# Bias tables asked for two heads ahead, and columns' rows with the last bias row, in a four-layer attention and recurrence trunk

## The chip, the cores and the metric

The kernel runs on one core of a Trainium2 chip. The metric is the device time of one execution in microseconds; of several executions the median counts. The engines are named as the profile names them: PE is TensorE (PEld its weight load), DVE is VectorE, ACT is ScalarE, POOL is GpSimd and SP is SyncE, here only a queue of DMAs.

## The reference

512 tokens of width 1024 go through two layers, each a token mixer and a gated feed-forward block (FFN) with a short convolution, all in float32, each between two RMS norms. The first layer's mixer is dilated attention with 8 heads in three groups, the second one's a gated linear recurrence (RG-LRU). What touches the change is the attention's bias and the convolutions' weights:

```python
m, valid, kidx = band_geometry(band)
bucket = t5_bucket(np.clip(m, 0, band) * dilation)
bias = jnp.transpose(bias_table.astype(jnp.float32)[bucket], (2, 0, 1))
...
logits = jnp.einsum('bxhnqd,bxhnkd->bxhnqk', qs, kk) * scale
logits = logits + bias[None, None, :, None]
mx = jnp.max(logits, axis=-1, keepdims=True)
p = jnp.exp(logits - mx)
s = jnp.sum(p, axis=-1, keepdims=True)
o = jnp.einsum('bxhnqk,bxhnkd->bxhnqd', p, vv) / s
```

A bias depends only on the distance of query and key, so that a head's bias is one row of numbers, shifted by one from query to query. The convolutions are depthwise: each channel has three (FFN) or four (recurrence) weights and a bias.

## The kernel before

Every float32 matrix is held as two float32r parts, a high one and the rest, and a product is three matmuls. The weights come from HBM in pieces of about 1 MB: `load` (L299) issues them on SP, ACT makes the high part (L240 in `pump`) and DVE the low one (L249 in `low_parts`). Eight such units may be live. For some products sums of two weight blocks are needed; `add_up` (L282) loads one block on SP (L292) and lets POOL add the other by an accumulating DMA into the same tile (L294).

The code is written in the order in which each engine works; no scheduler reorders it, and each engine keeps that order, so that an instruction that waits holds up all behind it on its engine. The order is interleaved by hand: after each block of matmuls, some 5.5 us of PE, `tick` (L351) lets every registered side generator take its next step and splits one or two weight units. A side's `yield n` means that it goes on n ticks later.

The attention (`attention`, L856) works through four pairs of heads twice. In the first round it projects queries, keys and values for group 0 and registers `local` (L1038) for two heads, which go on during the next pair's projections: in one tick the scores (PE, L1047), scores plus bias with their maximum (DVE, L1034) and exponentials (ACT, L1060); three ticks later the transposes (PE, L1069) and their copies; one tick later the product with the values (L1082). In the second round `strided` (L1089) does the same for groups 1 and 2 of a head together, and mixes the three groups.

The side `biases` (L864) runs in the first pairs. It makes for each of the three groups a row of bias values per head (matmul L875, copy L876, written to HBM at L877) and writes it 128 times into `skew` in HBM (L878), so that a DMA that reads it with a row step of one less than the row's length gets a head's bias table as a tile. `toeplitz` (L889) is that DMA, issued on POOL (L891) where a head's scores are emitted, into the tile `toe`, of which there are two buffers. After the third group `biases` loads three small constants and goes on into `feature_columns` (L705): it loads the convolutions' weights as rows (`column_rows`, L685, DMAs at L691 on SP), two ticks later turns them into columns by a PE transpose (`columns`, L695, transpose L698, copy L700), and for the recurrence computes constants from one of them by a chain of small DVE operations (L717 to L730). Then it does so for each of the two FFNs.

Most intermediate tiles are 128x512 float32 tiles of the pool `gp`, of which there are 30 buffers (`GEN_BUFS`). A tile's buffer is free after its last use, and a new tile takes a free one, the oldest as a rule. `dynamic_dma_scratch_size` (L1494) is the space in each SBUF partition in which POOL writes the descriptors of its DMAs, here 2048 bytes.

## Time and profile before

| | |
|---|---|
| median of 3 runs | 1486.01 us (1485.98 to 1488.6) |
| the profiled execution | 1485.73 us |
| its span, first to last instruction | 1484.0 us |
| PE busy | 1459.4 us (98%) |
| DVE busy | 931.1 us (63%) |
| ACT busy | 655.8 us (44%) |
| POOL busy | 78.0 us (5%) |
| mean granted TensorE clock | 0.994 |

All later times are microseconds from the span's start. The attention layer takes the first 540 us or so, the first FFN runs to about 930, the recurrence to about 1080, and the second FFN to the end. A row of the chain of waits has start, length and what ran; a row of the timeline has start, length, engine, line, operation, tiles (out<-in) and, in brackets, how long the engine sat idle before it and what ended that. A row of the windows has the stretch, then the busy time of PE, PEld, DVE, ACT and POOL with their counts, then granted clock, DMA share and GB/s. A releaser is inferred; where the engine named was done long before, it was another, often a DMA.

### The profile page before, as it was taken

The numbers are of one execution on the slowest core, as the hardware profiler recorded it, in microseconds if no ns is written. First come the engines' busy times: TensorE is split into PE (matmuls) and PEld (weight loads), VectorE is DVE, ScalarE is ACT, GpSimd is POOL, SyncE is SP. The second block draws the span as 40 slices with busy tenths as digits, with TensorE's granted clock in tenths as the row PEclk, the third lists the DMA queues.
The fourth block names the chain that finished last, engine by engine and source line by source line (L and its number), as shares of the span: only waits on it lengthen the run. The fifth ranks groups of instructions, "written<-read, shape, count | busy, mean of one in ns | idle before, by whom it ended". The sixth has DMA issues, their size and how long they took to land.

```text
span 1484.0 us, 19296 instructions
## 1 busy us (share of the span) xinstructions
PE 1459.4 (98%) x7625; PEld 1249.1 (84%) x7625; DVE 931.1 (63%) x1627; ACT 655.8 (44%) x1098; POOL 78.0 (5%) x91
## 2 busy tenths in 40 slices
PE   8999989999999999999999999999999999999998
PEld 6787868888888898999988888988798999888886
DVE  6365345255535588887877336877778888775333
ACT  5343234243434454454545224479554445544221
POOL 0101110111000000111000000000000011000000
PEclk9999989999999999999999999999999999999999
DMA  6664555736534343677645212331343667545101
GB/s 202 213 188 114 127 138 173 182 81 187 194 103 164 114 153 108 142 180 185 171 165 199 90 57 85 103 125 44 119 137 109 161 161 175 161 163 199 65 0 57
DMA packets 152651, 203.86 MB, mean 137 GB/s; under 512 B 5896, under 2 KB 129296, under 8 KB 152561
## 3 DMA queue, kind: packets, MB, share of 16 engines
q1 hardware_dynamic: 128064, 170.64, 34.2%
q0 software_dynamic: 24496, 31.99, 11.7%
q8 instruction: 60, 0.98, 0.3%
q14 instruction: 31, 0.25, 0.0%
HBM read 189.98 MB, written 17.34 MB: 140 GB/s over the span
## 4 chain that ended last, share of the span: by engine, by line
PE 85%; DVE 6%; ACT 4%; DMA 3%; issue 1%; SPq 0%; POOL 0%; DVEq 0%; ACTq 0%; POOLq 0%
PE ps L416 41%; PE acc L416 22%; PE vq L416 11%; PE vq L948 4%; PE v L922 2%; DVE wlo L249 2%; DVE xb L1286 1%; DMA raw<-in_attn_w_qkv_dram 1%; PE tr L465 1%; PE S L1111 1%; PE O L1082 1%; PE O L1179 1%; ACT whi L240 1%; PE S L1047 1%; DVE th L1338 1%
## 5 line engine op out<-in xcount | busy, mean ns | idle before, releaser
L416 PE MATMUL ps<-hT,whi 128*128 128x512 f32 (+1 forms) x2240 | 647.6, 374 | 0.8 <-ACT qk L902 0.7
L416 PEld LDWEIGHTS ps<-hT,whi 128*128 128x128 f32 x2240 | 405.7, 189 | 72.8 <-ACT qk L902 2.2
L416 PE MATMUL ps<-hT,wlo 128*128 128x512 f32 (+1 forms) x1120 | 416.7, 372 | 0.0
L249 DVE TENSOR_TENSOR wlo<-raw,whi 128x1024 fp32r<-128x1024 f32 x244 | 295.2, 1219 | 141.2 <-ACT whi L240 140.7
L240 ACT ACTIVATE whi<-raw 128x1024 fp32r<-128x1024 f32 x244 | 252.7, 1053 | 193.5 <-PE acc L416 124.4
L416 PEld LDWEIGHTS ps<-hT,wlo 128*128 128x128 f32 x1120 | 211.5, 189 | 37.2
L416 PE MATMUL acc<-whi,ahi 128*128 128x512 f32 x512 | 200.6, 392 | 1.1 <-ACT ahi L171 1.1
L416 PE MATMUL acc<-whi,alo 128*128 128x512 f32 x512 | 199.5, 390 | 0.0
L416 PE MATMUL acc<-wlo,ahi 128*128 128x512 f32 x512 | 199.2, 389 | 0.0
L750 DVE SCALAR_TENSOR_TENSOR u<-ps,cols,u 128x511 f32<-128x511 f32 (+1 forms) x128 | 95.7, 748 | 38.5 <-ACT u L746 36.2
L416 PEld LDWEIGHTS acc<-whi,ahi 128*128 128x128 f32 x512 | 96.1, 188 | 21.0 <-ACT ahi L171 1.5
L416 PEld LDWEIGHTS acc<-whi,alo 128*128 128x128 f32 x512 | 96.1, 188 | 20.6 <-DVE alo L172 0.4
L416 PEld LDWEIGHTS acc<-wlo,ahi 128*128 128x128 f32 x512 | 96.2, 188 | 19.5
L416 PE MATMUL vq<-T,whi 128*128 128x256 f32 x512 | 93.4, 283 | 0.0
L416 PEld LDWEIGHTS vq<-T,whi 128*128 128x128 f32 x512 | 81.4, 192 | 1.9
L240 ACT ACTIVATE whi<-sum 128x1024 fp32r<-128x1024 f32 x40 | 41.8, 1052 | 86.1 <-DMA sum<-in_attn_w_qkv_dram 60.6
L249 DVE TENSOR_TENSOR wlo<-sum,whi 128x1024 fp32r<-128x1024 f32 x40 | 48.5, 1220 | 44.8 <-ACT whi L240 44.8
L416 PE MATMUL vq<-T,wlo 128*128 128x256 f32 x256 | 72.4, 283 | 0.0
L760 ACT ACTIVATE u<-u 128x512 f32<-128x512 f32 x48 | 30.4, 632 | 92.2 <-DVE u L750 92.2
L416 PE MATMUL vq<-hT,whi 128*128 128x256 f32 x384 | 69.7, 283 | 0.0
L1034 DVE CUSTOM_DVE_ANT_0 L<-S,toe 128x128 f32<-128x128 f32 (+1 forms) x96 | 25.1, 320 | 63.4 <-DMA toe<-skew 31.3
L746 ACT ACTIVATE u<-ps,cols 128x512 f32<-128x512 f32 x64 | 49.0, 766 | 31.7 <-PE ps L416 31.7
(211 smaller groups left out, 1698.5 us busy)
## 6 DMA issues: line engine op xcount, KB each, us to landing
raw<-in_ffn_w_up_dram SPq DMA_DIRECT2D x40, 1024.0 KB
raw<-in_attn_w_qkv_dram SPq DMA_DIRECT2D x26, 1024.0 KB
raw<-in_ffn_w_down_dram SPq DMA_DIRECT2D x12, 1024.0 KB
raw<-in_ffn_w_down_dram SPq DMA_DIRECT2D x24, 512.0 KB
raw<-in_attn_w_qkv_dram SPq DMA_DIRECT2D x16, 512.0 KB
sum<-in_attn_w_qkv_dram POOLq DMA_DIRECT2D x16, 512.0 KB, 6.3
sum<-in_ffn_w_up_dram SPq DMA_DIRECT2D x16, 512.0 KB
sum<-in_ffn_w_up_dram POOLq DMA_DIRECT2D x16, 512.0 KB, 6.3
```

The source lines that it names most:

```text
L240: nc.scalar.activation(hi, raw, AF.Copy)
L249: nc.vector.tensor_tensor(lo, raw, hi.bitcast(F32), op=ALU.subtract)
L416: mm(dst, l[a], r[b], start=start and n == 0, stop=stop and n == 2)
L465: nc.tensor.transpose(ps[:, k * P : (k + 1) * P], xs[i][:, k * P : (k + 1) * P], ident)
L746: nc.scalar.activation(u, ps, AF.Identity, scale=cc[:, j : j + 1], bias=cc[:, 48 + j : 49 + j])
L750: nc.vector.scalar_tensor_tensor(u[:, d:], ps[:, : S - d], wc, u[:, d:], op0=ALU.mult, op1=ALU.add)
L760: nc.scalar.activation(u, u, AF.Gelu_apprx_tanh)
L922: mm(banks[t], hT[a][:, k, t * P : (t + 1) * P], W[b][:, k % 2, :], start=(k, a, b) == (0, 0, 0), stop=(k, a, b) == (KD - 1, 1, 0),)
L948: mm(banks[u], act(a)[:, 2 * j + k, u * P : (u + 1) * P], W[b][:, k, :], start=(j, k, n) == (0, 0, 0), stop=(j, k, n) == (1, 1, 2),)
L1034: nc.vector.tensor_tensor_reduce(dst, ps, bias, scale=1.0, scalar=3 * NEG, op0=ALU.add, op1=ALU.max, accum_out=mx)
L1047: mm(Sp[a // 2][:, o + lo : o + 256], q[hh][:, a * P : (a + 1) * P], k[hh][:, k0 : (a + 1) * P], start=True, stop=True)
L1082: mm(po[:, a * P : (a + 1) * P], pts[a, j], vtile(v, a - 1 + j, h % 4), start=j == js[0], stop=j == 1)
```

## The change

- `toeplitz` no longer loads one table into a tile that it is given. A list `tables` holds all 24 tables in the order of their use; each call asks for as many as there are buffers for (`TOE_BUFS`, now 3 instead of 2) and returns the oldest one asked. So the first call asks for three tables, and each later one for one table, two calls ahead of its use.
- The rows of the columns, all five tiles of them with their sixteen DMAs, are asked for in the step in which the third group's bias row is made (`g == 2`), four ticks earlier than the first ones before. `feature_columns` gets the loaded rows, and its ticks of waiting between loading and transposing are gone, so that the five transposes follow in three successive ticks.
- The general pool has 29 buffers instead of 30.
- The space for POOL's descriptors is 4096 bytes of each partition instead of 2048.

```diff
-GEN_BUFS = 30
-TOE_BUFS = 2
+GEN_BUFS = 29
+TOE_BUFS = 3
...
-    def feature_columns():
+    def feature_rows():
         v = lambda r: r.rearrange("(j p) -> j p", p=P)
         v2 = lambda r: r.rearrange("n (j p) -> (n j) p", p=P)
-        rows = column_rows(
+        yield column_rows(
             [(v(lru_conv_w[0, k]), 8) for k in range(4)]
             + [(v(lru_conv_b[0]), 8), (v2(lru_ga_b[0]), 8), (v2(lru_gx_b[0]), 8), (v(lru_lambda[0]), 8)]
         )
-        yield 2
-        cl = columns(*rows)
+        for layer in range(2):
+            cw, cb = ffn_conv_w[layer], ffn_conv_b[layer]
+            yield column_rows([(v(cw[0]), 48), (v(cw[1]), 48)])
+            yield column_rows([(v(cw[2]), 48), (v(cb), 48)])
+
+    def feature_columns(rows):
+        cl = columns(*rows.pop(0))
...
         for layer in range(2):
-            cw, cb = ffn_conv_w[layer], ffn_conv_b[layer]
-            rows = column_rows([(v(cw[0]), 48), (v(cw[1]), 48)]), column_rows([(v(cw[2]), 48), (v(cb), 48)])
-            yield 2
-            ffn_cols[layer] = [columns(*r) for r in rows]
+            ffn_cols[layer] = [columns(*rows.pop(0)) for _ in range(2)]
             yield 1
...
+                if g == 2:
+                    rows = list(feature_rows())
                 yield 3
...
-            yield from feature_columns()
-
-        def toeplitz(dst, g, h, n):
-            o = skew[g].offset + h * P * TOE + 127
-            nc.gpsimd.dma_start(dst, bass.AP(tensor=skew[g].tensor, offset=o, ap=[[TOE - 1, P], [1, n]]))
+            yield from feature_columns(rows)
+
+        tables = [(0, h, 256) for h in range(HEADS)]
+        tables += [(g, h, P) for h in range(6) for g in (1, 2)] + [(g, h, P) for g in (1, 2) for h in (6, 7)]
+        asked = []
+
+        def toeplitz(*which):
+
+            while tables and len(asked) < TOE_BUFS:
+                g, h, n = tables.pop(0)
+                T = gp.tile([P, 256], F32, tag="toe", name=nm("toe"), bufs=TOE_BUFS)
+                o = skew[g].offset + h * P * TOE + 127
+                src = bass.AP(tensor=skew[g].tensor, offset=o, ap=[[TOE - 1, P], [1, n]])
+                nc.gpsimd.dma_start(T[:, :n], src)
+                asked.append(((g, h), T))
+            key, T = asked.pop(0)
+            assert key == which
+            return T
...
         def local(h, hh, q, k, v):
-            T = gp.tile([P, 256], F32, tag="toe", name=nm("toe"), bufs=TOE_BUFS)
-            toeplitz(T, 0, h, 256)
+            T = toeplitz(0, h)
...
-                T = gp.tile([P, 256], F32, tag="toe", name=nm("toe"), bufs=TOE_BUFS)
-                toeplitz(T[:, :P], gi + 1, h, P)
+                T = toeplitz(gi + 1, h)
...
-    nc = _bacc.Bacc("TRN2", target_bir_lowering=False, num_devices=1, dynamic_dma_scratch_size=2048)
+    nc = _bacc.Bacc("TRN2", target_bir_lowering=False, num_devices=1, dynamic_dma_scratch_size=4096)
```

## The prediction

> **What bounds the kernel now.** I read the page first, then the list of PE's waits, then the chain of waits around each of them, and last the queues of the engines that the change touches.

> ```profile
> span 1484.0 us, 19296 instructions
> PE 1459.4 (98%) x7625; PEld 1249.1 (84%) x7625; DVE 931.1 (63%) x1627; ACT 655.8 (44%) x1098; POOL 78.0 (5%) x91
> PE PT L1069 <- ACT L L1060: 6.6, 1, 6.6
> PE cols L698 <- DMA st<-in_ffn_conv_w_dram: 2.2, 1, 2.2
> PE c L1165 <- DVE qk L904: 0.8, 1, 0.8
> ```

> The run is bound by TensorE: it idles 1484.0 - 1459.4 = 24.6 us, the most that an edit leaving its matmuls alone can win by idle time. Three of its few waits (time in all, count, longest) hang on what the diff touches: transposes of a local head's weights (L1069), transposes of the columns' rows (L698), and the small product at L1165 in the first strided head.

> Place one, by the chain of waits (start, length, what), with the last matmul ahead of it:

> ```profile
> 129.79 0.39 PE L922 MATMUL v<-whi,hT 128*128 128x512 f32 x1
> 125.18 5.10 DMA raw<-in_attn_w_qkv_dram
> 130.67 1.66 DMA st<-in_ffn_conv_w_dram
> 132.34 0.34 PE cols L698
> 132.68 1.69 PE PT L1069 x7
> 134.36 6.08 PE ps L416 x24
> 142.00 0.77 PE PT L1069 x7
> 142.76 5.47 PE ps L416 x24
> 132.00:134.00 2.00, 1.66 (x8) 1.57 (x9) 1.93 (x4) 0.93 (x2) 0.00 (x0) 0.53 0.14 37
> ```

> PE ends its value product at 129.79 + 0.39 = 130.18 and stands until the rows land (the chain hangs on the last of the small loads, which SP issued behind a 1 MB weight load). Afterwards the granted clock, the third number from the end in the window row, is 0.53: the same seven transposes and 24 matmuls take 1.69 and 6.08 us, and at full clock, eight us later, 0.77 and 5.47.

> Place two:

> ```profile
> 177.35 1.68 PE L1047 MATMUL S<-qk,qk 128*128 128x128 f32 x8
> 189.56 5.28 issue
> 194.85 0.76 POOL sum L294
> 195.60 5.74 DMA toe<-skew
> 201.48 0.29 DVE L1034 CUSTOM_DVE_ANT_0 L<-S,toe 128x128 f32<-128x128 f32 x1 [20.36 <-DMA toe<-skew]
> 203.05 1.97 ACT L L1060 x8
> 196.58 0.39 PE L416 MATMUL ps<-hT,wlo 128*128 128x512 f32 x1
> 203.60 2.16 PE L1069 MATMUL PT<-ident,L 128*128 128x128 f32 x7 [6.63 <-ACT L L1060]
> 206.50 7.69 PE ps L416 x24
> 204.00:206.00 2.00, 1.75 (x7) 0.86 (x6) 1.70 (x12) 2.00 (x7) 0.19 (x1) 0.50 0.22 66
> ```

> Head 4's scores S are there at 177.35 + 1.68 = 179.03. VectorE cannot add the bias: its table stands in GpSimd's queue behind two accumulating loads, the second of which starts only after 5.28 us without a visible releaser. The table lands after 201, VectorE has idled 20.36 us and blocked everything behind it, the exponentials follow, and PE stands from 196.97 to 203.60. Its clock is then 0.50.

> **The change part by part.** *Tables two heads ahead (three buffers).* Nothing is added: 24 table loads before and after. What moves is when they are asked for.

> ```profile
> 113.17 1.62 POOL L891 DMA_DIRECT2D toe<-skew  x2
> 141.32 1.33 POOL L294 DMA_DIRECT2D sum<-in_attn_w_qkv_dram  x1 [26.52 <-ACT qk L902]
> DMA to landing us min/median/max: 2.1/4.4/8.5
> 119.34 0.29 DVE L1034 CUSTOM_DVE_ANT_0 L<-S,toe 128x128 f32<-128x128 f32 x1 [10.97 <-PE S L1047]
> ```

> The call of head 2 will ask for head 4 and that of head 3 for head 5, where today the two tables of heads 2 and 3 are asked, at 113.17. With the longest landing, 8.5 us, head 4's table is there at about 122, 57 us before S. Head 4 at place two then runs: VectorE is done with the step before at 201.48 - 20.36 = 181.12, scores and maxima take 203.05 - 201.48 = 1.57, exponentials 1.97, done at about 184.7. PE wants them at 196.97, so 12 us are spare and the stall is gone. Without it, place two costs 0.77 + 5.47 = 6.24 us instead of (206.50 + 7.69) - 196.97 = 17.22: **11.0 us won**.

> Each new ask waits for the maxima of the call before it, whose buffer it takes. Queued behind it on GpSimd are the accumulating loads; the nearest one behind an early ask starts at 141.32, 28 us after 113.17, and at place two the two loads stand ahead of the asks. VectorE finishes a head's maxima 1.57 us after it starts them, so these waits cost nothing; if that cover went, an accumulating load would be late by what the wait lasts, and ACT, which splits in order, with it.

> Head 2 gains as well: VectorE's 10.97 us ahead of 119.34 end 6.2 us after its table was asked, which is the table's landing and not the later S that the row names. I count that at nothing, since PE works through it.

> The first strided head is the third place:

> ```profile
> 309.13 1.68 POOL L891 DMA_DIRECT2D toe<-skew  x2
> 316.26 0.29 DVE L1034 CUSTOM_DVE_ANT_0 L<-S,toe 128x128 f32<-128x128 f32 x1 [11.18 <-PE vq L948]
> ```

> Again the scores start a landing (7.1 us) after the ask, and VectorE's backlog runs from there into the 0.8 us wait at L1165. Tables asked during heads 6 and 7 take these 7 us out: **0.8 us won**.

> *Columns' rows with the last bias row.* Sixteen small loads move on SP, from behind the weight load of 125.18 (and two later places) to the step in which the third bias row is made.

> ```profile
> 83.73 0.37 SPq L322 DMA_DIRECT2D raw<-in_attn_w_qkv_dram  x1
> 92.84 0.37 SPq L322 DMA_DIRECT2D raw<-in_attn_w_qkv_dram  x1
> 130.67 1.24 SPq L691 DMA_DIRECT2D st<-in_ffn_conv_w_dram  x3
> 163.62 2.06 SPq L691 DMA_DIRECT2D st<-in_ffn_conv_w_dram  x3
> 104.13 2.00 ACT L240 ACTIVATE whi<-raw 128x1024 fp32r<-128x1024 f32 x2
> 134.96 0.22 DVE L700 COPY cols<-cols 128x64 f32<-128x64 f32 x1
> 138.75 0.17 DVE L730 TENSOR_SCALAR pad<-c 128x8 f32<-128x8 f32 x1
> ```

> In SP's order they fall between the weight loads of 83.73 and 92.84, where SP has 92.84 - 84.10 = 8.7 us free. An issue takes 1.24/3 = 0.41 to 2.06/3 = 0.69 us, sixteen 6.6 to 11.0, so the load of 92.84 and the loads behind it slip by 0 to 2.3 us. With a landing like the 5.10 us above it is there at 97.9 and ACT splits it from 104.13: 6.2 us cover the slip; what went beyond them would come out of ACT's and then PE's time. The rows are then read at the step of head 3's scores, about 117, twenty us after their issue. Place one costs 0.77 + 5.47, and 0.17 for the rows' own transpose at full clock, 6.41 us instead of (134.36 + 6.08) - 130.18 = 10.26: **3.9 us won**. VectorE's chain of small operations on these columns, 138.92 - 134.96 = 4.0 us, moves ahead of head 3's scores; VectorE is then earlier by the idle time ahead of 119.34, and head 3's transposes come only at 142.00, so it costs nothing.

> [...]

> *Descriptor space 4 KB.* If the 5.28 us are a wait for space, the second accumulating load starts right after the first and lands up to 5 us earlier. PE shows no wait for these sums, so I price it at 0; the bounds are 0 and, against, whatever two such loads at once take from a weight load, whose nearest row is again the 6.2 us of cover.

> *29 general buffers.* No instruction changes; an allocation takes a buffer freed one step later. I take 0; its upper bound is the second rival.

> **Sum.** 11.0 + 3.9 + 0.8 = 15.7 (unrounded 15.6). I keep back 0.6, somewhat less than one wait like that of L1165, because PE will reach everything behind 130 earlier than today: 15.0. The profiled execution took 1485.73 us, 1.73 outside its span; the median of the runs shown, 1486.01, is 0.28 above it. Forecast 1486.0 - 15.0 = **1471.0 us**.

> **The rivals.** *ACT's wait for the sums takes the table's place.* Behind head 5's exponentials ACT splits the summed tile and only then copies head 4's transposed weights.

> ```profile
> DMA to landing us min/median/max: 5.8/6.3/10.3
> ```

> If the larger space does nothing, the second load still starts at 194.85 and lands after 6.3 us at 201.1; a split like that of 104.13 (1.0 us) and the copy (about 0.5) follow at 202.6, and PE wants the copy 6.24 us after 196.97, at 203.2. That fits; with the longest landing, 10.3, PE would stand 3.4 us and lose as much as place one (1.7) by the clock: 1476. For it speaks that ACT idles on such sums elsewhere; against, that it needs two misfortunes. A slip of the rows that leaves place one as it is gives 1475. I give both together 0.16.

> [...] That the small loads behind an accumulating load are issued at once, and only a second accumulating one waits, speaks for space all the same.

> *Slower: the general buffers run out in the FFN.* Counted in the code from first to last use, general tiles reach 29 at once near the end of each FFN's up-projections, one below today's 30 and all of the new pool.

> ```profile
> L750 DVE SCALAR_TENSOR_TENSOR u<-ps,cols,u 128x511 f32<-128x511 f32 (+1 forms) x128 | 95.7, 748 | 38.5 <-ACT u L746 36.2
> 740.00:760.00 20.00, 20.00 (x123) 17.93 (x122) 15.64 (x22) 10.08 (x12) 0.00 (x0) 1.00 0.39 130
> ```

> If each of the last two pairs' evacuations (12 in a layer, 24 in all) waited one VectorE step of 0.75 us and PE with it, 18 us would be lost: 1471 + 18 = 1489. It decides where evacuation is as slow as PE; the window shows VectorE at 15.64 and ACT at 10.08 of 20 us beside a full PE, with eight PSUM banks between them. Chance 0.03.

> *Nothing changes:* another wait ends just as late at both places, some weight load behind ACT's order, and the time stays at 1486. Against it: at place two all of ACT and VectorE waits for this one table. Chance 0.05.

> **How the numbers follow.** The forecast, 1469 to 1473.5, has 0.76; the partial cases to 1477 have 0.16. The range 1469 to 1477 leaves out the last two rivals and some tails. A measurement here tells about 0.2%, 3 us, from no change; every case but the last two lies beyond it: faster 0.92, within 0.05, slower 0.03.

> **What would show it.** Right: the waits of L1069 and L698 gone from PE's list, the granted clock 1.00 from 130 to 140 and from 190 to 210, VectorE no longer waiting for toe, the row loads issued around 85 to 95, the pairs of accumulating loads 1 to 2 us apart. Wrong: a wait of PE behind ACT's split of a sum near 195, a weight load late near 100, or idle PE with half clock in the FFN around 780.

## The result, and the profile after

The changed kernel takes **1471.06 us** (median of 4 runs, 1470.15 to 1472.11) beside 1485.99 us for the kernel before on the same chip: a ratio of 0.9898, 95% interval 0.9881 to 0.9915. Its profiled execution took 1470.15 us. From its page (PE is busy for 1455.4 us, 99%) and its list of PE's waits (us in all, times, longest):

```profile
span 1468.4 us, 19295 instructions
...
PE tr L465 <- DVE xs L501: 2.0, 2, 1.8
...
PE acc L416 <- ACT ahi L171: 1.3, 1, 1.3
PE v L939 <- ACT hT L469: 1.1, 1, 1.1
PE c L1180 <- DVE s L1182: 0.2, 1, 0.2
```

All three places are gone from the list, and no wait has taken their part. (A line 15 to 17 above one of before is the same line.) Where the time was won shows at four products that both kernels do. Three rows of each kernel are from the chain of waits, in which a product starts some 0.16 us later than in the timeline (214.19 there, 214.03 here). Head 4's scores are compared in the timeline, where they start at 177.35 before. Before:

```profile
214.19 1.56 PE O L1082 x14
...
303.11 1.78 PE S L1111 x16
...
353.90 1.78 PE O L1179 x16
```

After:

```profile
131.25 0.77 PE PT L1085 x7
132.02 5.48 PE ps L416 x24
...
199.79 1.56 PE O L1098 x14
...
288.71 1.78 PE S L1126 x16
...
338.08 1.78 PE O L1194 x16
```

```profile
173.95 1.68 PE L1063 MATMUL S<-qk,qk 128*128 128x128 f32 x8
```

Head 4's scores start at 173.95 instead of 177.35: 3.4 us won up to there, by place one. Its output product starts at 199.79 instead of 214.19, 14.4 us earlier, so place two brought 11.0. Up to the first strided head's scores nothing is added (303.11 - 288.71 = 14.4), and behind its tables the output product is 353.90 - 338.08 = 15.8 us earlier: place three brought 1.4. The span is 15.6 us shorter. PE never stands in the windows in which the steps of places one and two run now, and its granted clock (third number from the end) stays full, so that the seven transposes and 24 matmuls of place one take 0.77 and 5.48 us instead of 1.69 and 6.08:

```profile
130.00:140.00 10.00, 10.00 (x61) 8.77 (x60) 6.90 (x12) 4.99 (x9) 2.68 (x2) 1.00 0.28 41
190.00:200.00 10.00, 10.00 (x51) 8.41 (x50) 3.71 (x5) 1.74 (x3) 0.00 (x0) 1.00 0.56 185
```

POOL's and SP's queues after (start, length, then what; in brackets the idle time before and its releaser):

```profile
106.44 2.69 POOL L294 DMA_DIRECT2D sum<-in_attn_w_qkv_dram  x2 [13.85 <-DMA sum<-in_attn_w_qkv_dram]
```

```profile
84.88 1.46 SPq L691 DMA_DIRECT2D st<-in_lru_conv_w_dram  x4
...
93.77 0.47 SPq L322 DMA_DIRECT2D raw<-in_attn_w_qkv_dram  x1
...
117.86 0.38 SPq L322 DMA_DIRECT2D raw<-in_attn_w_qkv_dram  x1
```

The two accumulating loads now stand in one row, without 5 us between them. The rows go out from 84.88. And the weight load that stood at 125.18 goes at 117.86, 7.3 us earlier, though nothing in the diff touches it. That last row is the thread to pull.

### The profile page after: what moved, and what is told of

The parts are those of the page before. It is cut to its first block, busy times and chain, and to the rows that moved or that the text cites. A ratio compares the mean times of both kernels' runs of the same rounds, so it can differ in the third digit from the quotient of the medians.

```text
span 1468.4 us, 19295 instructions
## 1 busy us (share of the span) xinstructions
PE 1455.4 (99%) x7625; PEld 1249.3 (85%) x7625; DVE 933.5 (64%) x1627; ACT 658.1 (45%) x1098; POOL 78.2 (5%) x91
## 4 chain that ended last, share of the span: by engine, by line
PE 94%; DVE 2%; ACT 2%; DMA 1%; issue 0%; SPq 0%; DVEq 0%
PE ps L416 46%; PE acc L416 22%; PE vq L416 11%; PE vq L965 5%; PE v L939 3%; PE gate L416 1%; PE tr L465 1%; PE S L1126 1%; PE O L1098 1%; PE S L1063 1%; PE O L1194 1%; DMA raw<-in_attn_w_qkv_dram 1%; DVE wlo L249 1%; PE PT L1085 0%; PE PT L1175 0%
## 5 line engine op out<-in xcount | busy, mean ns | idle before, releaser
L416 PE MATMUL ps<-hT,whi 128*128 128x512 f32 (+1 forms) x2240 | 645.4, 373 | 0.0
L416 PEld LDWEIGHTS ps<-hT,whi 128*128 128x128 f32 x2240 | 404.7, 189 | 70.9 <-issue 1.3
L416 PE MATMUL ps<-hT,wlo 128*128 128x512 f32 (+1 forms) x1120 | 415.9, 371 | 0.0
L240 ACT ACTIVATE whi<-raw 128x1024 fp32r<-128x1024 f32 x244 | 253.1, 1053 | 183.5 <-PE acc L416 124.4
L416 PEld LDWEIGHTS ps<-hT,wlo 128*128 128x128 f32 x1120 | 211.1, 188 | 36.8
L416 PE MATMUL acc<-whi,ahi 128*128 128x512 f32 x512 | 200.6, 392 | 1.3 <-ACT ahi L171 1.3
L416 PE MATMUL acc<-whi,alo 128*128 128x512 f32 x512 | 199.6, 390 | 0.0
L416 PE MATMUL acc<-wlo,ahi 128*128 128x512 f32 x512 | 199.3, 389 | 0.0
L752 DVE SCALAR_TENSOR_TENSOR u<-ps,cols,u 128x511 f32<-128x511 f32 (+1 forms) x128 | 95.7, 748 | 49.6 <-ACT u L748 47.3
L416 PEld LDWEIGHTS acc<-whi,ahi 128*128 128x128 f32 x512 | 96.2, 188 | 21.2 <-ACT ahi L171 1.7
L416 PEld LDWEIGHTS acc<-whi,alo 128*128 128x128 f32 x512 | 96.1, 188 | 20.5 <-DVE alo L172 0.4
L416 PEld LDWEIGHTS acc<-wlo,ahi 128*128 128x128 f32 x512 | 96.2, 188 | 19.5
L416 PE MATMUL vq<-T,whi 128*128 128x256 f32 x512 | 93.4, 283 | 0.0
L416 PEld LDWEIGHTS vq<-T,whi 128*128 128x128 f32 x512 | 81.4, 192 | 1.9
L416 PE MATMUL vq<-T,wlo 128*128 128x256 f32 x256 | 72.5, 283 | 0.0
L416 PE MATMUL vq<-hT,whi 128*128 128x256 f32 x384 | 69.7, 283 | 0.0
L240 ACT ACTIVATE whi<-sum 128x1024 fp32r<-128x1024 f32 x40 | 41.7, 1049 | 47.2 <-DMA sum<-in_attn_w_qkv_dram 47.2
L416 PEld LDWEIGHTS vq<-hT,whi 128*128 128x128 f32 x384 | 60.4, 192 | 0.6
L249 DVE TENSOR_TENSOR wlo<-sum,whi 128x1024 fp32r<-128x1024 f32 x40 | 48.5, 1219 | 15.6 <-ACT whi L240 15.6
```

What stands on the lines that cost most here:

```text
L240: nc.scalar.activation(hi, raw, AF.Copy)
L249: nc.vector.tensor_tensor(lo, raw, hi.bitcast(F32), op=ALU.subtract)
L416: mm(dst, l[a], r[b], start=start and n == 0, stop=stop and n == 2)
L752: nc.vector.scalar_tensor_tensor(u[:, d:], ps[:, : S - d], wc, u[:, d:], op0=ALU.mult, op1=ALU.add)
```

## The experiments

The theory on record gave each place its own cause: the tables win places two and three, the rows' move wins place one, the space nothing. The rival is one cause: VectorE waits 11 us for head 2's table (119.34 in the trace of before), and ScalarE's splits, the weight load of 125.18 and the rows behind it all hang on that. Beside the three groups of runs the kernel before took 1487.18, 1486.25 and 1486.65 us.

**Tables alone.** The change without the rows' move and with the old space:

```diff
-                if g == 2:
-                    rows = list(feature_rows())
...
-dynamic_dma_scratch_size=4096
+dynamic_dma_scratch_size=2048
```

> Only the tables two heads ahead (three table buffers, 29 general ones); rows and descriptor space as before. Theory of the prediction, parts add: places two and three go, place one stays with PE waiting about 2 us for the columns' rows near 130 at half clock; 1486.0 - 11.0 - 0.8 = 1474.2, and the wait of L698 is still in PE's list. Rival, one cause: head 2's early table frees VectorE near 112 instead of 119, so that SP's weight load of 125 and the rows behind it go out some 7 us earlier and are there before PE wants them; then place one goes too and the time is that of the whole change, 1471, with no wait of L698.

Measured: 1471.65 us (1470.93 to 1471.8), ratio 0.9893 [0.988, 0.9906]. SP's queue:

```profile
117.96 0.38 SPq L322 DMA_DIRECT2D raw<-in_attn_w_qkv_dram  x1
118.44 1.47 SPq L691 DMA_DIRECT2D st<-in_lru_conv_w_dram  x4
```

The weight load goes at 117.96 and the unmoved rows right behind it, and PE finds them there. All three places are won without the rows' move.

**Rows alone.** The kernel before with the rows' move and nothing else:

```diff
+                if g == 2:
+                    rows = list(feature_rows())
```

> Only the columns' rows asked with the last bias row; two table buffers asked at use, 30 general buffers, 2 KB. Prediction: place one goes (3.9 us), places two and three stay; 1482.1, PE still waits 6 to 7 us at the transposes of head 4. Rival: PE, earlier by 3.9 us, waits that much longer for head 4's table, whose time is set by the sums' loads and not by PE; then the 3.9 us are given back at place two and the time is 1486.

Measured: 1491.76 us (1488.76 to 1492.83), ratio 1.0023 [1.0014, 1.0032]: slower. PE's waits, POOL's queue and VectorE's order:

```profile
PE PT L1073 <- ACT L L1064: 4.2, 1, 4.2
PE PT L1073 <- DVE s L1038: 3.6, 1, 3.6
...
PE ps L416 <- DVE cols L700: 3.2, 1, 3.2
```

```profile
116.97 1.30 POOL L294 DMA_DIRECT2D sum<-in_attn_w_qkv_dram  x1 [9.02 <-issue]
```

```profile
132.07 0.22 DVE L700 COPY cols<-cols 128x64 f32<-128x64 f32 x1
...
135.92 0.28 DVE L1038 CUSTOM_DVE_ANT_0 L<-S,toe 128x128 f32<-128x128 f32 x1
```

At place one PE no longer waits for the rows but for VectorE's part of head 3's scores (3.6 us) and then for VectorE's copies of the columns out of PSUM (3.2 us). Two things differ from the trace of before: POOL stands 9.0 us ahead of the second accumulating load instead of 5.2, so the tables come later; and VectorE works off the recurrence constants (132.07 to 135.92) ahead of head 3's scores.

**Space alone.** The kernel before with 4 KB and 29 general buffers:

```diff
-dynamic_dma_scratch_size=2048
+dynamic_dma_scratch_size=4096
```

> Only 4 KB of descriptor space, with 29 general buffers to make room for it; tables and rows as before. If the 5.3 us between two accumulating loads are a wait for space, the second one starts 1.3 us after the first, head 4's table is asked 4 us earlier, and place two shrinks from 11.0 to about 5 us with less or no half clock; 1480. [...]

Measured: 1475.75 us (1474.74 to 1477.32), ratio 0.992 [0.9907, 0.9933]. POOL at place two, and at place one PE and the chain of waits:

```profile
187.87 1.29 POOL L294 DMA_DIRECT2D sum<-in_attn_w_qkv_dram  x1 [0.56 <-DMA sum<-in_attn_w_qkv_dram]
188.63 1.72 POOL L891 DMA_DIRECT2D toe<-skew  x2
```

```profile
134.56 0.24 PE L698 MATMUL cols<-ident,st 64*128 64x64 f32 x1 [3.12 <-DMA st<-in_ffn_conv_w_dram]
```

```profile
109.03 12.08 DMA toe<-skew
...
127.03 5.62 DMA raw<-in_attn_w_qkv_dram
...
133.03 1.52 DMA st<-in_ffn_conv_w_dram
```

The 5 us between the loads (5.07 at place two in the timeline of before) hung on the descriptor space: with 4 KB they are 0.56. Head 4's table is asked at 188.63 instead of 195.60, and the wait for its exponentials is gone from PE's list. So is the 0.8 us of place three, with no table asked early. Place one stays: head 2's table is asked at 109.03 instead of 113.17, but takes 12.1 us to land, so that VectorE starts at 121.24 instead of 119.34. Here the chain names the table itself, and leads from it over the weight load at 127.03 to the rows that PE waits for. So space and early tables are substitutes at places two and three, but not at place one.

**The change with the old space.**

```diff
-dynamic_dma_scratch_size=4096
+dynamic_dma_scratch_size=2048
```

> The whole change but with 2 KB of descriptor space as before. Prediction: the space is worth 0 once the tables come early, since PE waits for no sum; 1471.0, with the 5 us gaps between accumulating loads back. Rival: ACT's in-order wait for the later sums reaches PE at place two, 1473 to 1476.

Measured: 1474.21 us (1471.5 to 1479.38), ratio 0.9917 [0.99, 0.9934]. POOL, ACT and PE at place two, then VectorE and PE at place one:

```profile
197.18 1.29 POOL L294 DMA_DIRECT2D sum<-in_attn_w_qkv_dram  x1 [8.92 <-issue]
```

```profile
203.31 1.06 ACT L240 ACTIVATE whi<-sum 128x1024 fp32r<-128x1024 f32 x1 [13.02 <-DMA sum<-in_attn_w_qkv_dram]
```

```profile
204.79 0.94 PE L1098 MATMUL O<-v,PT 128*128 128x128 f32 x6 [1.39 <-ACT PT L1088]
```

```profile
125.77 0.17 DVE L724 TENSOR_SCALAR s<-s 128x8 f32<-128x8 f32 x1 [4.88 <-ACT s L723]
```

```profile
134.48 0.73 PE L416 MATMUL ps<-hT,whi 128*128 128x512 f32 x2 [1.66 <-DVE cols L700]
```

At place two this is the prediction's first rival row by row: the late second load, the split of its sum, the copy behind the split (at 204.27), PE standing 1.39 us for it. The same happens at place one, which no expectation had: ACT waits for a sum until 123.58, the exponential that the recurrence constants need comes behind that split, VectorE stands 4.88 us for it with head 3's scores behind, and PE 1.66 us for the columns' copies. With the rows moved, the space is worth 3 us, by these rows about half of it at each place.

**Tables and space, without the rows' move**, and **rows and space, without the early tables**:

```diff
 # tables and space: the change without these lines
-                if g == 2:
-                    rows = list(feature_rows())
 # rows and space: the change with the old toeplitz and two table buffers
```

> The tables two ahead and the larger descriptor space, without the rows' move. Theory: the tables alone remove all three waits of TensorE (head 2's early table frees VectorE and ScalarE, so that the weight load ahead of the rows is issued at about 118 instead of 125), and the space has nothing left to win where the rows stay behind that load: 1471.0 to 1471.9, within 1 us of the tables alone (1471.65) and of the whole change. The pairs of accumulating loads lie 1 to 2 us apart and TensorE still has no wait of the rows. Rival: the larger space keeps a gain of its own (it brought 11 us on the kernel before by itself), so it is under 1470. Second rival: the rows' move does win something beside the tables, then this one is 2 us or more above the whole change, 1473 or more.

> The rows' move, the larger space and 29 general buffers, with each table still asked by the head that uses it. Theory: the rows' move costs time by what it does to the second accumulating load (9 us behind the first instead of 5), and that is a wait for descriptor space; with 4 KB it is gone, so that here the move wins place one (3.9 us) on top of the space alone (1475.75), and only place three is left: 1472 to 1473. Rival: the move costs time by VectorE's small operations on the constants, 4 us ahead of head 3's scores, whatever the space; then this is not below the space alone, 1475 to 1480, with a wait of TensorE near 136 for the scores.

Measured: 1470.66 us (1470.35 to 1471.79), ratio 0.9897 [0.9882, 0.9912], and 1481.54 us (1480.97 to 1481.96), ratio 0.9967 [0.9955, 0.998]. The first equals the whole change: the rows' move adds nothing there. The second is 5.8 us above the space alone, although its accumulating loads stand together and its tables are asked at 109.71 (VectorE starts on head 2's scores at 121.57, as with the space alone). Its VectorE and PE:

```profile
129.23 0.22 DVE L700 COPY cols<-cols 128x64 f32<-128x64 f32 x1
...
133.09 0.29 DVE L1038 CUSTOM_DVE_ANT_0 L<-S,toe 128x128 f32<-128x128 f32 x1
```

```profile
133.78 1.24 PE L1073 MATMUL PT<-ident,L 128*128 128x128 f32 x7 [2.10 <-DVE s L1038]
138.69 1.22 PE L416 MATMUL ps<-hT,whi 128*128 128x512 f32 x2 [3.68 <-DVE cols L700]
```

The rival expectation held in its cause, and the time is 1.5 us above its range: the constants ahead of head 3's scores cost time with the larger space too.

**The rows one bias row earlier**, on the kernel before:

```diff
+                if g == 1:
+                    rows = list(feature_rows())
```

> The kernel before with the rows' loads moved alone, as in the run that was slower (1491.76), but with the second bias row instead of the third, some 20 us earlier, where the sums' first loads have no small load just ahead. Theory: the move alone was slower because the small loads pushed the sums' first loads and the weight load behind them into the first accumulating load; here the first accumulating load starts at about 104 and the second about 110.7 as in the kernel before, the tables of heads 2 and 3 are asked at about 113, and the rows are there when TensorE asks: place one is won and place two stays, 1482 to 1484. Rival: the 4 us of VectorE's operations on the constants ahead of head 3's scores are what costs, so this is no better than the kernel before: 1487 to 1492.

Measured: 1490.57 us (1486.46 to 1493.13), ratio 1.0024 [1.0014, 1.0035]. No better than the later place, as the rival had it. It does not acquit SP's slip, though: the small loads now stood ahead of other weight loads, the sums' first loads still went late (95.77; traces without the move have 93.26 to 94.99), and POOL stood 7.4 us ahead of the second accumulating load.

**The rows early, but used at the old step**, with the larger space and on the kernel before:

```diff
     def feature_columns(rows):
+        yield 2
         cl = columns(*rows.pop(0))
...
+            yield 2
             ffn_cols[layer] = [columns(*rows.pop(0)) for _ in range(2)]
```

> As the run with the rows' move and the larger space (1481.54), but the columns are made from the rows at the old step again: the loads stay early, the transposes and VectorE's 4 us of constants go back behind head 3's scores. Theory: the early use of the rows is what cost 6 us against the space alone (1475.75), since it put those constants ahead of head 3's scores; here both are gone, the constants and the wait for the rows: 1470.8 to 1472.5, with no wait of TensorE between 125 and 145. Rival: the early loads themselves cost (SyncE's later weight loads, the shared DMA engines), so this stays at 1476 or more.

> As the run with the rows' move alone (1491.76), but with the columns made at the old step. Theory: two costs were in it, the constants ahead of head 3's scores, and tables of heads 2 and 3 that land 5 us later because the accumulating loads start later; here only the second is left. Head 3's scores then run at about 132 and TensorE stands about 2 us for the exponentials instead of for the rows: as the kernel before or a little under 1486.25, 1484 to 1487. Rival: late tables cost nothing here and place one is won in full: 1482 to 1483. Second rival: the early loads are all of the cost, and it stays near 1491.

Measured: 1478.18 us (1477.84 to 1479.38), ratio 0.995 [0.9937, 0.9962], and 1490.42 us (1486.59 to 1492.61), ratio 1.0025 [1.0012, 1.0037]. The theory missed both times. With the larger space 3.4 of the 5.8 us come back, but place one is not won; the times are those of the rivals, yet in the traces PE stands for VectorE and not for a load. PE and VectorE with the larger space:

```profile
130.67 0.27 PE L698 MATMUL cols<-ident,st 64*128 64x64 f32 x1
...
141.01 2.29 PE L1088 MATMUL O<-v,PT 128*128 128x128 f32 x9 [3.68 <-DVE PT L1080]
```

```profile
136.41 0.22 DVE L700 COPY cols<-cols 128x64 f32<-128x64 f32 x1
...
140.27 0.68 DVE L1080 COPY PT<-PT 128x512 f32<-128x512 f32 x1
```

PE takes the rows without waiting, and ten us later stands 3.68 us for VectorE's copy of head 3's transposed weights, which comes behind the constants. On the old space it is the same, 2.92 us, and the output product starts no earlier than in the kernel before (the trace is of the fastest of the seven executions, 1486.59). From the kernel before and from this one:

```profile
140.28 1.72 PE L1082 MATMUL O<-v,PT 128*128 128x128 f32 x14
```

```profile
140.56 1.83 PE L1088 MATMUL O<-v,PT 128*128 128x128 f32 x14 [2.92 <-DVE PT L1080]
```

So the wait for the rows at place one stood in front of a second one, about as costly: VectorE was late by itself, since it had waited for head 2's table.

**Head 2's table alone early**, on the kernel before with three table buffers and 29 general ones:

```diff
-            T = gp.tile([P, 256], F32, tag="toe", ...)
-            toeplitz(T, 0, h, 256)
+            for j in range(3) if h == 0 else [h] if h > 2 else []:
+                early[j] = gp.tile([P, 256], F32, tag="toe", ...)
+                toeplitz(early[j], 0, j, 256)
+            T = early.pop(h)
```

> The kernel before with three table buffers, 29 general buffers and one table asked early: head 2's, along with those of heads 0 and 1. All others are asked by the head that uses them, the rows are not moved, the space is 2 KB. Theory: VectorE's wait of 11 us ahead of head 2's scores is what holds back ScalarE's split, and by it the weight load of 125 and the rows behind it; with head 2's table there, that load goes at about 118, the rows land before TensorE asks, and place one is won (3 to 4 us) while place two and place three stay: 1481.5 to 1483.5. Rival: the rows' place hangs on the rows' place in SyncE's order alone, so one early table wins nothing: 1485.5 to 1487. A third: head 3's table, still behind the accumulating loads, takes head 2's place and TensorE waits for its exponentials: 1484 to 1486.

Measured: 1481.26 us (1479.92 to 1482.37), ratio 0.9968 [0.9956, 0.9981], about 5 us under the kernel before. SP and the windows around places one and two:

```profile
117.66 0.38 SPq L322 DMA_DIRECT2D raw<-in_attn_w_qkv_dram  x1
```

```profile
120.00:160.00 40.00, 40.00 (x200) 33.46 (x199) 22.59 (x51) 14.63 (x27) 4.35 (x4) 1.00 0.49 115
160.00:220.00 60.00, 54.41 (x251) 44.60 (x250) 24.71 (x47) 19.02 (x35) 5.73 (x7) 0.94 0.49 132
```

One early table wins all of place one (PE full from 120 to 160) and leaves place two, with 4.8 us of PE's wait there. This settles it: place one's cause is head 2's table. All the traces agree: VectorE starts on head 2's scores between 111.57 and 124.47, and in each of the fourteen kernels SP issues the weight load that stood at 125.18 in the kernel before 5.8 to 6.2 us later.

**Tables one head ahead** instead of two, and **29 general buffers alone**:

```diff
 # the change
-TOE_BUFS = 3
+TOE_BUFS = 2
 # the kernel before
-GEN_BUFS = 30
+GEN_BUFS = 29
```

> The whole change with two table buffers instead of three, so that each table is asked one head ahead. Theory: one head ahead already puts the asks in front of the accumulating loads (head 4's is asked with head 3, near 114, 60 us before its scores), so this is the whole change over again: 1470.5 to 1471.7, no wait of TensorE for a table. Rival: with one table in hand the asks of the later heads fall behind the accumulating loads of the steps between, VectorE waits for a table again at a strided head or at head 5, and 1 to 5 us come back: 1472 to 1476.

> The kernel before with 29 general buffers instead of 30 and nothing else. Theory: no tile waits for a buffer, so no change, 1485.5 to 1487. Rival: the pool runs out near the end of each feed-forward layer's up-projections, and evacuations and TensorE wait there: up to 18 us more, 1490 to 1504, with idle TensorE behind 740.

Measured: 1470.08 us (1469.6 to 1470.69), ratio 0.9891 [0.9877, 0.9904], and 1487.48 us (1484.62 to 1492.93), ratio 1.0005 [0.9993, 1.0017]. One head ahead is enough: the third buffer buys nothing that can be measured. The 29 buffers end half a microsecond above the expected range, and the ratio tells nothing from no change; PE stays full where they might run out:

```profile
700.00:1000.00 300.00, 300.00 (x1544) 257.68 (x1543) 193.37 (x287) 134.72 (x199) 6.04 (x7) 1.00 0.38 121
```

All eight combinations in one table (us; the last column is what the rows' move does, by the medians and, since they come from different groups of runs, also by the ratios to the kernel before):

| tables | space | rows not moved | rows moved | move |
|---|---|---|---|---|
| at use | 2 KB | 1487.18 | 1491.76 | +4.6 (+3.4) |
| at use | 4 KB | 1475.75 | 1481.54 | +5.8 (+7.0) |
| ahead | 2 KB | 1471.65 | 1474.21 | +2.6 (+3.6) |
| ahead | 4 KB | 1470.66 | 1471.06 | +0.4 (+0.1) |

## Why the prediction was right, and where it was not

The time was right (1471.0 forecast), and so were the sizes: 11.0, 3.9 and 0.8 us forecast for the three places, 11.0, 3.4 and 1.4 found. One attribution was wrong, and it reaches into two other steps.

- *Place two by the tables:* right, cause and size. Tables alone do it.
- *Place one by the rows' move, 3.9 us:* this step failed. The price was right (from the end of the last value product to the first output product 10.10 us before, 6.25 after), the cause was not: the tables win it alone, and the move by itself makes the kernel slower. The prediction had seen that head 2's 11 us of idle VectorE would go and counted that "at nothing, since PE works through it". PE works through it, but VectorE then runs late, and with it the split, the load of 125.18, the rows, and the copy of head 3's weights. Read back from the rows, the chain of before leads from their load to the issue at 125.18, and from there to 119.34.
- *The constants ahead of head 3's scores cost nothing:* true only under the tables and the larger space together. The prediction named that cover (VectorE earlier by the idle time ahead of 119.34) but not the price without it: with the space but no tables the move costs 5.8 us, 3.4 of which go when the rows are used at the old step. With the tables but the old space the chain stands 4.88 us for ACT, and PE 1.66 us for what follows.
- *Space at 0:* true only beside the early tables and unmoved rows (1471.65 to 1470.66, less than can be told). By itself it wins about 11 us, at places two and three, since the table that PE's wait hung on stood behind the second accumulating load; the prediction quoted that chain and still looked only for a wait of PE for the sums. Beside the moved rows it is worth 3 us.
- *The slip of the weight load, 0 to 2.3 us:* 0.9 found (93.77 against 92.84), but the first accumulating load slips by 2.3 (106.44 against 104.18), which the prediction did not follow to POOL. One pair of traces does not size it: those without the move have 103.96 to 106.14, those with it 105.91 to 106.75.
- *Place three, 0.8:* too small, and the cause is one of two that do: the space alone takes this wait out as well. PE's list of before shows 0.8 us of it, the two ends of the chain 1.4. From the transposes ahead of the wait to the output product PE takes 18.5 us before and 17.4 after, 1.1 us; the other 0.3 lie between the first scores and these transposes, where no row shows a wait of PE.
- *ACT's wait for the sums:* the mechanism is real and stands in the run with the old space, with 1.39 us at place two and, over the constants, 1.66 at place one, which the rival did not have; in the change the larger space keeps it away. That the loads' own wait hangs on the space is shown at place two: the second one stood 5.07 us with 2 KB and 0.56 with 4 KB alone.
- *29 buffers:* nothing, as priced.
- *0.6 us kept back:* no new wait came that it stood for. The profiled executions are 15.6 us apart, as the sum without it, and the medians 14.9, as with it.

That the forecast came out to a tenth of a microsecond is in part luck, and says little about its terms: place one's price was bounded by PE's own gap, so any cause that closed the gap would have given the same number. What stays open is how the remaining 2.4 us of the move with the larger space divide between VectorE's copy and the clock, and how much SP's slip costs by itself; the run meant to free it of the slip did not.

## What to carry to other kernels

A wait that names a DMA or a small load tells what came last, not why: follow its issue back on its own queue, and ask whether the engine that you free elsewhere is what held it. Before crediting an edit with a gap, look for the next thing that would be late there; here two waits about equally costly stood in one gap, and removing the first won nothing. Where several parts of a change touch one chain, run them alone and in pairs: here two of them were substitutes, and one did harm that only the others together covered.

## What the runs showed of the hardware

```profile
132.00:132.50 0.50, 0.16 (x1) 0.18 (x1) 0.50 (x2) 0.50 (x2) 0.00 (x0) 0.64 0.18 51
135.50:136.00 0.50, 0.50 (x4) 0.41 (x3) 0.25 (x2) 0.50 (x4) 0.00 (x0) 0.95 0.00 0
200.00:200.50 0.50, 0.00 (x0) 0.00 (x0) 0.00 (x0) 0.00 (x0) 0.00 (x0) 0.90 1.15 365
210.50:211.00 0.50, 0.50 (x3) 0.45 (x2) 0.50 (x2) 0.50 (x1) 0.00 (x0) 0.86 1.08 379
```

The windows beside them show 1.00 or 0.50. By an estimate from these means, 0.64 between full and half clock puts the first fall at 132.14, and likewise the rise at 135.55, the second fall at 200.40 and its rise at 210.64. The distances are 3.41, 68.26 (20 times 3.413) and 10.24 (3 times 3.413). Read the same way, place one's fall and rise lie 3.41 us apart with the space alone (means of 0.80 from 135.50 to 136.00 and 0.79 from 139.00 to 139.50), 6.83 with the rows one bias row earlier (0.63 from 136.50, 0.54 from 143.00) and 10.24 with the rows alone (0.61 from 136.00, 0.65 from 146.00). In the trace of before the first fall came 2.0 us after PE's last matmul, and in the 3.41 us up to that fall (from 128.73) PE was busy for 42%, to 130.18. In the run with the rows used late on the old space, 2.92 us of idle PE brought no fall at all:

```profile
138.00:140.00 2.00, 0.00 (x0) 0.00 (x0) 1.73 (x12) 1.46 (x3) 0.00 (x0) 1.00 0.00 0
140.00:142.00 2.00, 1.44 (x12) 1.44 (x13) 2.00 (x3) 0.00 (x0) 0.00 (x0) 1.00 0.06 12
```

That run's later fall and rise (mean clock 0.79 from 200.50 to 201.00 and 0.97 from 211.00 to 211.50) stand at 200.79 and 211.03. Counted back from there in steps of 3.413 us, its gap from 137.64 to 140.56 is shared by two steps, in which PE was busy for 50% and 65%. The author's estimate from these two gaps is that a gap of 2 to 3 us costs the half clock or not by where it falls among the steps. That would explain why the kernels with both gaps spread by 4 to 8 us from run to run and those with neither by 1 to 2; it was not tested, and the wait in the next paragraph, which differs between executions too, is a rival.

**With 2 KB, the wait between the first two accumulating loads was longer where a weight load followed at once.** POOL stood 5.0 to 5.3 us between them where SP's next weight load came 1.5 to 2.65 us after the first of them had started (the kernel before, tables alone, head 2's table early, the rows used late on the old space). It stood 7.4 and 7.5 us where that load came 1.2 us after (one bias row earlier; 29 buffers alone), and 9.0 us where it came 0.8 and 0.9 us after (the change with the old space; rows alone). It is not the rows' move alone: the 29 buffers leave the rows where they were. The trace of that kernel is of its slowest execution, 1492.93 us, in which PE stands 4.6 us for the rows instead of 2.2. Why the wait grew was not tried.
